# Rows scaled by ScalarE and added in device memory, and squares summed by VectorE, at the end of a transformer layer

## Chip, cores and metric

The kernel runs on one core of a Trainium2 chip. The metric is the device time of one execution in microseconds (us); smaller is better. A time is the median of several runs; beside it stands one profiled execution, whose trace is what the text quotes. Engines are named as in the profile: PE (TensorE), DVE (VectorE), ACT (ScalarE), POOL (GpSimd) and SP (SyncE, here used only to issue transfers). The transfers that SP and ACT issue go through hardware queues, those of POOL through the software queue.

## The reference

One layer of a hybrid encoder on 512 positions of width 1024, in float32. Its first half makes x1 from x. Its second half is a gated MLP with a convolution over positions, and a normalised residual; the end of that second half is where the change lies:

```python
def _rmsnorm(x, g):
    y = x * lax.rsqrt(jnp.mean(x * x, axis=-1, keepdims=True) + EPS)
    return y * g
...
h2 = _rmsnorm(x1, g_pre_ffn)
z  = _conv_gated_mlp(h2, w_up, conv_w, conv_b, w_down)     # ends with (512 x 2816) @ (2816 x 1024)
y  = x1 + _rmsnorm(z, g_post_ffn)
```

For one row of z the end is thus: a sum of 1024 squares, its mean plus EPS to the power -0.5 (one number per row, called the scale here), the product of z, the scale and g_post_ffn, and the sum with x1.

## The kernel before

The 512 positions are four **tokens** in the kernel's words, blocks of 128 rows, one row per partition (NT = 4). The 1024 columns are two halves of 512 (n = 0 and 1). Everything is float32, and a product is made exact enough by splitting each operand in a high and a low part and adding three matmuls.

x1 is made in `norms` (L1138) at some 425 to 455 us, and each half of each token (128 x 512) goes to a scratch tensor in device memory by a transfer of POOL (L1155), since it is needed again only at the very end.

The last product (by `w_down`) is made in two passes, one per half of the output columns. Each pass combines seven products of quarter blocks per step (`products`, a scheme with fewer multiplications; L1358) into the accumulators M1 to M8, and some rest of the contraction is added directly by `add_whole` (L1378), 24 matmuls of 128 x 256 for each token and pass. The first pass leaves its results (columns 0 to 511) in the tiles `c4`. During the second pass `first_share` (L1436) squares and sums those columns on ACT and puts their product with g_post_ffn into the tile `zg[t]`, both well before the end.

What follows the second pass is the **tail**, in `token` (L1452), called for the tokens 0, 2, 1, 3 in this order. For each: `add_whole` finishes the accumulators on PE, first the one for columns 512 to 767 (12 matmuls), then the one for columns 768 to 1023. For each of these two pieces i = 0, 1 of 128 x 256:

- `sums(i)`: DVE adds accumulator and a tile into `z` (L1470), and ACT squares it with a sum along the row (L1472, an ACTIVATE and the read of its accumulator).
- `weighted(i)`: DVE multiplies `z` by g_post_ffn into `zs` (L1477).

Then `first_sum` (L1480) and `scale` (L1487) add up the four sums of squares on DVE, tiny instructions of 128 x 1, and POOL raises the result to the power -0.5 into `qr` (L1488, the pow). `rows` (L1513) makes the result: one DVE instruction per half multiplies `zg` or `zs` by the scale and adds x1, loaded back by SP (L1458), all of it 128 x 512 (the second half of the last token in two pieces of 256), and SP and ACT issue the transfers to the output (L1523). `rows` of one token is called within `token` of the next one, so that it does not wait for its own pow; only the last token's rows stand alone at the end (L1546).

Within one engine, instructions run in the order of the queue. A scheduler sets that order by priority, except where `keep_in_program_order` pins an instruction to the place in which the code gives it, or `issue_after` holds it behind another.

Of the kernel before, what the change touches and what calls it, by code (L numbers as in the profile page):

```python
# [12 lines left out]
AF = mybir.ActivationFunctionType  # L13
# [3 lines left out]
D = 1024  # L17
# [9 lines left out]
NW = 146  # L27
SV0, U0, GATE0, GATE1 = 24, 32, 40, 72
LOOK = 4
NBLK = 66  # L30
WARM = 17
RES_OUT = 6
# [20 lines left out]
def tile_block(ctx: ExitStack, tc, xT, x, wall, par, cs, wsp, bsp, gpost, gffn, out):  # L53
# [33 lines left out]
    def halves(n):  # L87
        return [blk(n=n), blk(n=n)]
# [1361 lines left out]
    ahead = []  # L1450

    def token(t):  # L1452

        if not ww:
            ww.extend([w_get(), w_get()])
        xt = halves("x1")
        for n in range(2):
            nc.sync.dma_start(xt[n], x1[t][n])  # L1458
        add_whole(m, t, (0, 1), ww, True)
        z, zs_ = blk(n="z"), blk(n="zs")  # L1460
        last, ahead[:] = list(ahead), []
        banks = (((M2, e1), (M3, xx)), ((M4, uu), (M8, yy)))[t // 2]
        halves_ = slice(0, 256), slice(256, 512)
        end = t in (1, NT - 1)
        pin = tc.keep_in_program_order if end else (lambda i: i)

        def sums(i):
            b, e = banks[i]
            f = halves_[t % 2]
            pin(v.tensor_add(z[:, halves_[i]], m[b][:, f], e[:, f]))  # L1470
            j = tmp("junk")
            nc.scalar.activation(  # L1472
                out=j[:, :256], in_=z[:, halves_[i]], func=AF.Square, scale=D ** -0.5, accum_out=qn[t][:, 2 + i : 3 + i]
            )

        def weighted(i):
            pin(v.tensor_mul(zs_[:, halves_[i]], z[:, halves_[i]], gpf[1][:, halves_[i]]))  # L1477

        def first_sum():
            pin(v.scalar_tensor_tensor(  # L1480
                out=qn[t][:, 0:1], in0=qn[t][:, 2:3], scalar=EPS, in1=qn[t][:, 0:1], op0=ALU.add, op1=ALU.add
            ))

        sc, s_2 = small("qr", 1, 4), small("qs", 1, 4)

        def scale():
            pin(v.tensor_add(s_2, qn[t][:, 0:1], qn[t][:, 3:4]))  # L1487
            nc.gpsimd.tensor_tensor(out=sc, in0=s_2, in1=nhalf[:, 0:1], op=ALU.pow)  # L1488

        sums(0)  # L1490
        if t == NT - 1:
            weighted(0)
            sums(1)
            first_sum()
            rows(*last, (0,), pin)
            scale()
            rows(*last, (1,), pin)
            weighted(1)
        else:
            weighted(0)  # L1500
            first_sum()
            if end:
                rows(*last, (0,), pin)
            sums(1)
            if last:
                rows(*last, (1,) if end else (0,), pin)
            scale()
            weighted(1)
            if last and not end:
                rows(*last, (1,))  # L1510
        ahead[:] = t, xt, zs_, sc

    def rows(t, xt, zs_, sc, which, pin=lambda i: i):  # L1513

        zt = (zg[t], zs_)
        for i, (a, b) in enumerate(((0, 512), (512, 768), (768, 1024)) if t == NT - 1 else ((0, 512), (512, 1024))):
            if a // S in which:
                f = slice(a % S, a % S + b - a)
                o = zt[a // S][:, f]
                pin(v.scalar_tensor_tensor(  # L1520
                    out=o, in0=o, scalar=sc, in1=xt[a // S][:, f], op0=ALU.mult, op1=ALU.add
                ))
                (nc.sync, nc.scalar)[i % 2].dma_start(out[t, :, a:b], o)  # L1523

    def after6():
        v.tensor_add(uu, m[M6], e1)
# [16 lines left out]
    m[M8] = ps()  # L1543
    for t in (2, 1, 3):
        token(t)
    rows(*ahead, (0, 1))  # L1546


def _parts(a, n, w):
# [129 lines left out]
```

## Time and profile before

| | us |
|---|---|
| median of 3 runs | 783.69 (783.55 to 783.72) |
| profiled execution, its own time | 784.33 |
| its span | 782.6 |
| around the span | 1.73 |
| PE busy | 774.5 (99%) |
| DVE busy | 639.5 (82%) |
| ACT busy | 485.2 (62%) |
| POOL busy | 103.5 (13%) |

The span is what the trace covers, from 0 to 782.6 us; all positions in the text count from its start. The rest of the execution's own time, 1.73 us, lies outside. The profiled execution took 0.64 us more than the median, so a prediction made on the span is carried to the median by its difference. A granted clock of 0.997 in the profiled execution says that PE was hardly throttled.

A row of a timeline gives the start, the duration, engine, line, operation, output and inputs, and in square brackets how long the engine had been idle and what it waited for. Consecutive DVE instructions that don't depend on each other overlap by some 0.08 us in these rows; one that waits for the result of the row ahead starts about 0.03 us after that one's end.

### The profile page before, as it was taken

Reading aid. Unit: us, or ns where it says so; the run is one execution under the profiler, and the core shown is the slowest. Engines: PE = TensorE matmul, PEld = TensorE weight load, DVE = VectorE, ACT = ScalarE, POOL = GpSimd, SP = SyncE. Lnnn points to the kernel's source line nnn. Section 1 sums busy time; section 2 is a strip of 40 time slices with the busy share of each in tenths; the row PEclk is TensorE's granted clock in tenths of the full one; section 3 lists DMA queues with packets and bytes.
Section 4 is the critical chain, followed back from the end, with each engine's and each line's share of the span. In section 5 each row is a group of like instructions: output and inputs, shape, how many; then the busy total and the mean of one; then the engine's idle time right before and its main releaser. Section 6 shows DMA issues by size and latency. Waiting matters only on the chain.

```text
span 782.6 us, 13472 instructions
## 1 busy us (share of the span) xinstructions
PE 774.5 (99%) x5139; PEld 720.7 (92%) x5139; DVE 639.5 (82%) x1093; ACT 485.2 (62%) x878; POOL 103.5 (13%) x132
## 2 busy tenths in 40 slices
PE   9999999999999999999999999999999999999996
PEld 8888998998999999999998998999999998999996
DVE  6567987789789988877765679989999889886987
ACT  7555568688466766644454686657777568644542
POOL 0040001130021102033211200001111012200001
PEclk9999999999999999999999999999999999999998
DMA  8783224453223233233459120435555375733344
GB/s 288 271 246 102 81 82 162 108 122 108 81 91 126 82 122 121 83 110 106 138 171 337 54 81 28 124 107 141 142 148 149 108 199 111 171 114 107 109 162 162
DMA packets 35889, 104.80 MB, mean 134 GB/s; under 512 B 4400, under 2 KB 6320, under 8 KB 35824
## 3 DMA queue, kind: packets, MB, share of 16 engines
q1 hardware_dynamic: 27936, 87.81, 34.0%
q0 software_dynamic: 7024, 14.95, 9.0%
q10 hardware_dynamic: 864, 1.18, 0.4%
q8 instruction: 40, 0.66, 0.4%
q14 instruction: 25, 0.20, 0.1%
HBM read 91.34 MB, written 4.19 MB: 122 GB/s over the span
## 4 chain that ended last, share of the span: by engine, by line
PE 92%; DVE 3%; DMA 3%; issue 1%; ACT 0%; POOLq 0%; DVEq 0%; POOL 0%; ACTq 0%
PE ps L926 24%; PE ps L300 12%; PE ps L302 12%; PE ps L301 12%; PE ps L1372 7%; PE ps L755 5%; PE ps L634 4%; PE ps L636 4%; PE ps L635 4%; DMA raw<-wall 3%; PE ps L1109 2%; PE ps L1108 2%; PE ps L1107 2%; DVE dl L119 1%; PE ps L997 1%
## 5 line engine op out<-in xcount | busy, mean ns | idle before, releaser
L119 DVE TENSOR_TENSOR wl<-raw,wh 128x1024 fp32r<-128x1024 f32 (+1 forms) x84 | 96.0, 1152 | 54.3 <-issue 19.1
L100 ACT ACTIVATE wf<-raw 128x512 fp32r<-128x512 f32 x140 | 85.6, 625 | 67.3 <-PE ps L301 19.4
L926 PE MATMUL ps<-sh,wf 128*128 128x256 f32 x640 | 117.4, 276 | 0.1
L119 DVE TENSOR_TENSOR wf<-raw,wf 128x512 fp32r<-128x512 f32 x140 | 107.0, 774 | 9.2 <-ACT wf L100 8.6
L926 PEld LDWEIGHTS ps<-sh,wf 128*128 128x128 f32 x640 | 101.9, 192 | 1.1 <-ACT sig L100 0.5
L100 ACT ACTIVATE wh<-raw 128x1024 fp32r<-128x1024 f32 (+2 forms) x88 | 84.8, 977 | 28.5 <-DMA raw<-wall 14.0
L300 PE MATMUL ps<-h2h,wh 128*128 128x512 f32 (+1 forms) x256 | 90.6, 354 | 0.0
L301 PE MATMUL ps<-h2l,wh 128*128 128x512 f32 (+1 forms) x256 | 90.4, 353 | 0.0
L302 PE MATMUL ps<-h2h,wl 128*128 128x512 f32 (+1 forms) x256 | 90.4, 353 | 0.0
L926 PE MATMUL ps<-sl,wf 128*128 128x256 f32 x320 | 88.0, 275 | 0.0
L926 PEld LDWEIGHTS ps<-sl,wf 128*128 128x128 f32 x320 | 61.4, 192 | 0.4
L1372 PE MATMUL ps<-dh,fh 128*128 128x256 f32 x216 | 59.6, 276 | 0.3 <-DVE yy L1409 0.3
L1372 PE MATMUL ps<-dl,fh 128*128 128x256 f32 x216 | 59.5, 275 | 0.0
L1372 PE MATMUL ps<-dh,fl 128*128 128x256 f32 x216 | 59.4, 275 | 0.0
L100 ACT ACTIVATE dh<-raw 128x768 fp32r<-128x768 f32 (+1 forms) x36 | 33.6, 950 | 33.8 <-DVE raw L231 15.2
L302 PEld LDWEIGHTS ps<-h2h,wl 128*128 128x128 f32 x256 | 48.6, 190 | 5.1
L301 PEld LDWEIGHTS ps<-h2l,wh 128*128 128x128 f32 x256 | 48.6, 190 | 4.5
L300 PEld LDWEIGHTS ps<-h2h,wh 128*128 128x128 f32 x256 | 48.6, 190 | 4.5
L926 PE MATMUL ps<-xh,wf 128*128 128x256 f32 x288 | 52.2, 275 | 0.0
L636 PE MATMUL ps<-wh,xl 128*128 128x512 f32 x128 | 48.5, 379 | 0.0
L635 PE MATMUL ps<-wl,xh 128*128 128x512 f32 x128 | 48.5, 379 | 0.0
L634 PE MATMUL ps<-wh,xh 128*128 128x512 f32 x128 | 48.5, 380 | 0.0
(343 smaller groups left out, 2171.6 us busy)
## 6 DMA issues: line engine op xcount, KB each, us to landing
raw<-wall SPq DMA_DIRECT2D x144, 512.0 KB, 3.7
x<-x SPq DMA_DIRECT2D x24, 256.0 KB, 6.0
fl<-gp POOLq DMA_DIRECT2D x12, 256.0 KB, 3.8
swap<-qkraw POOLq DMA_DIRECT2D x16, 128.0 KB, 4.8
x<-x POOLq DMA_DIRECT2D x8, 256.0 KB, 2.3
fl<-fs POOLq DMA_DIRECT2D x8, 256.0 KB, 4.3
xT<-xT SPq DMA_DIRECT2D x7, 256.0 KB, 5.0
xT<-xT POOLq DMA_DIRECT2D x4, 256.0 KB, 4.1
```

Of the source, the lines that this page charges most:

```text
L100: return nc.scalar.activation(out=o, in_=i, func=AF.Copy)
L119: low[0] = nc.vector.tensor_sub(lo, src, as32(hi)).ins
L300: nc.tensor.matmul(o, ah, bh, start=start, stop=False, skip_group_check=skip)
L301: nc.tensor.matmul(o, ah, bl, start=False, stop=False, skip_group_check=skip)
L302: pe_last[0] = nc.tensor.matmul(o, al, bh, start=False, stop=stop, skip_group_check=skip).ins
L634: nc.tensor.matmul(acc[t], xh[k][:, c], turns(wh[:, f]), start=k == 0, stop=False)
L635: nc.tensor.matmul(acc[t], xh[k][:, c], turns(wl[:, f]), start=False, stop=False)
L636: part_end[0] = nc.tensor.matmul(acc[t], xl[k][:, c], turns(wh[:, f]), start=False, stop=k == KD - 1)
L755: nc.tensor.matmul(bank[t], a_[:, c], turns(w_[:, f]), start=first and k == i == 0, stop=last and k == 3 and i == 2, skip_group_check=True,)
L926: self.last = nc.tensor.matmul(o, w_[:, c], a_, start=first and k == n == 0, stop=k == 3 and n == 2, skip_group_check=True,)
L1107: nc.tensor.matmul(o, ah, turns(bh), start=k == 0, stop=False)
L1372: nc.tensor.matmul(o, a_[:, c], turns(w_[:, f]), start=j == t == i == 0, stop=j == DP - 1 and i == 2 and n not in (M2, M3, M4), skip_group ...
```

## The change

- **x1 of some rows goes to the output itself.** `norms` writes the halves in `BY_ACT` (both halves of tokens 0 and 2, the first half of token 1) into the output tensor, where x1 then stands until the tail; the other three go to the scratch tensor as before.
- **Those rows are finished by ACT and a transfer that adds.** `scaled_rows`: ACT multiplies the 128 x 512 tile by the scale in place, and POOL issues a transfer to the output with `accum_op=ADD`, which adds it to the x1 that lies there. Their load of x1, the DVE instruction and the transfer of SP or ACT go.
- **The squares of tokens 0, 2 and 1 are summed by DVE** (`squares`: a `tensor_tensor_reduce`, two instructions on the engine: the product with its sum, and the read of the accumulator). The sum starts from the value so far (`scalar=`), so the tiny additions go; EPS is added in `first_share`. For token 3 the first piece is still squared by ACT, the second by DVE.
- **The order at the end of the tail is written anew** for DVE, ACT and POOL.

```diff
+BY_ACT = (0, 0), (0, 1), (2, 0), (2, 1), (1, 0)
...
-            nc.gpsimd.dma_start(x1[t][n], xt[n])
+            nc.gpsimd.dma_start(out[t, :, n * S : (n + 1) * S] if (t, n) in BY_ACT else x1[t][n], xt[n])
...
-        v.tensor_add(qn[t][:, 0:1], qn[t][:, 2:3], qn[t][:, 3:4])
+        v.scalar_tensor_tensor(
+            out=qn[t][:, 0:1], in0=qn[t][:, 2:3], scalar=EPS, in1=qn[t][:, 3:4], op0=ALU.add, op1=ALU.add
+        )
...
-        xt = halves("x1")
+        xt = [None if (t, n) in BY_ACT else blk(n="x1") for n in range(2)]
         for n in range(2):
-            nc.sync.dma_start(xt[n], x1[t][n])
+            if xt[n]:
+                nc.sync.dma_start(xt[n], x1[t][n])
...
+        def squares(i):
             j = tmp("junk")
-            nc.scalar.activation(
-                out=j[:, :256], in_=z[:, halves_[i]], func=AF.Square, scale=D ** -0.5, accum_out=qn[t][:, 2 + i : 3 + i]
-            )
+            pin(v.tensor_tensor_reduce(
+                out=j[:, :256], in0=z[:, halves_[i]], in1=z[:, halves_[i]], scale=1.0 / D, scalar=qn[t][:, i : i + 1],
+                op0=ALU.mult, op1=ALU.add, accum_out=(qn[t][:, 1:2], s_2)[i],
+            ))
...
+        half(0)
+        if t == NT - 1:
+            j = tmp("junk")
+            squared = nc.scalar.activation(
+                out=j[:, :256], in_=z[:, halves_[0]], func=AF.Square, scale=D ** -0.5, accum_out=qn[t][:, 2:3]
+            ).ins
+            weighted(0)
+            with tc.issue_after(squared):
+                scaled_rows(*ahead, 0)
+            rows(*ahead, 1, pin)
+        else:
+            squares(0)
+            weighted(0)
+        half(1)
+        if t == NT - 1:
+            pin(v.tensor_add(qn[t][:, 1:2], qn[t][:, 0:1], qn[t][:, 2:3]))
+        squares(1)
+        power = nc.gpsimd.tensor_tensor(out=sc, in0=s_2, in1=nhalf[:, 0:1], op=ALU.pow).ins
+        weighted(1)
+        if t == 1:
+            with tc.issue_after(power):
+                scaled_rows(*kept, 1, True)
+        if t % 2 == 0:
+            scaled_rows(t, xt, zs_, sc, 0)
+            if t:
+                kept[:] = t, xt, zs_, sc
+                nc.scalar.activation(out=zs_, in_=zs_, func=AF.Copy, scale=sc)
+            else:
+                scaled_rows(t, xt, zs_, sc, 1)
+        ahead[:] = t, xt, zs_, sc
+
+    def scaled_rows(t, xt, zs_, sc, n, done=False):
+
+        o = (zg[t], zs_)[n]
+        if not done:
+            nc.scalar.activation(out=o, in_=o, func=AF.Copy, scale=sc)
+        nc.gpsimd.dma_start(out[t, :, n * S : (n + 1) * S], o, accum_op=ALU.add)
+
+    def rows(t, xt, zs_, sc, n, pin=lambda i: i):
+
+        o = (zg[t], zs_)[n]
+        parts = ((0, 256), (256, 512)) if t == NT - 1 and n else ((0, 512),)
+        for i, (a, b) in enumerate(parts):
             pin(v.scalar_tensor_tensor(
-                out=qn[t][:, 0:1], in0=qn[t][:, 2:3], scalar=EPS, in1=qn[t][:, 0:1], op0=ALU.add, op1=ALU.add
+                out=o[:, a:b], in0=o[:, a:b], scalar=sc, in1=xt[n][:, a:b], op0=ALU.mult, op1=ALU.add
             ))
...
+            (nc.scalar if n and i == 0 else nc.sync).dma_start(out[t, :, n * S + a : n * S + b], o[:, a:b])
```

Three places of the engines' queues show what moves. First DVE's queue from token 3's first piece to the end, before. `z_8895` and `zs_8896` are token 3's, `zg_8436` and `zs_8849` token 1's, `zg_8564` token 3's first half, `q_8180` its sums of squares, `qs_8898` the sum handed to POOL:

```order
L1470 TENSOR_TENSOR z_8895<-ps_8241,e_8182 128x256
L1477 TENSOR_TENSOR zs_8896<-z_8895,gpf_8249 128x256
L1470 TENSOR_TENSOR z_8895<-ps_8772,e_8184 128x256
L1480 SCALAR_TENSOR_TENSOR q_8180<-q_8180 128x1
L1520 SCALAR_TENSOR_TENSOR zg_8436<-zg_8436,qr_8850,x_1463_8820 128x512
L1487 TENSOR_TENSOR qs_8898<-q_8180 128x1
L1520 SCALAR_TENSOR_TENSOR zs_8849<-zs_8849,qr_8850,x_1464_8821 128x512
L1477 TENSOR_TENSOR zs_8896<-z_8895,gpf_8249 128x256
L1520 SCALAR_TENSOR_TENSOR zg_8564<-zg_8564,qr_8897,x_1471_8867 128x512
L1520 SCALAR_TENSOR_TENSOR zs_8896<-zs_8896,qr_8897,x_1472_8868 128x256 x2
```

The same place after the change; ISA is the `tensor_tensor_reduce` and the read of its accumulator, `z_8879`, `zs_8880`, `qs_8882` are token 3's, `zs_8838` token 1's, and line numbers are those of the changed kernel:

```order
L1473 TENSOR_TENSOR z_8879<-ps_8241,e_8182 128x256
L1483 TENSOR_TENSOR zs_8880<-z_8879,gpf_8249 128x256
L1528 SCALAR_TENSOR_TENSOR zs_8838<-zs_8838,qr_8839,x_1459_8811 128x512
L1473 TENSOR_TENSOR z_8879<-ps_8770,e_8184 128x256
L1500 TENSOR_TENSOR q_8180<-q_8180 128x1
L1477 ISA junk_8893,qs_8882<-z_8879,q_8180 128x256
L1477 ISA qs_8882 128x1
L1483 TENSOR_TENSOR zs_8880<-z_8879,gpf_8249 128x256
L1528 SCALAR_TENSOR_TENSOR zg_8564<-zg_8564,qr_8881,x_1466_8851 128x512
L1528 SCALAR_TENSOR_TENSOR zs_8880<-zs_8880,qr_8881,x_1467_8852 128x256 x2
```

Of token 1's two row instructions one is left, and it stands ahead of the addition that makes token 3's last piece of `z`, where both stood behind it; between the sum for POOL and the last rows only the weighted product is left.

Second, POOL's queue from the first pow of the tail, after the change (before, the four pow stand there alone, one behind the other). The tokens in the order of the four `qr` are 0, 2, 1, 3; `zg_8372` and `zs_8740` are token 0's, `zg_8500` and `zs_8796` token 2's, `zg_8436` token 1's:

```order
L1502 TENSOR_TENSOR qr_8741<-qs_8742,nhalf 128x1
L1521 DMA out<-zg_8372 128x512
L1521 DMA out<-zs_8740 128x512
L1502 TENSOR_TENSOR qr_8797<-qs_8798,nhalf 128x1
L1521 DMA out<-zg_8500 128x512
L1502 TENSOR_TENSOR qr_8839<-qs_8840,nhalf 128x1
L1521 DMA out<-zs_8796 128x512
L1521 DMA out<-zg_8436 128x512
L1502 TENSOR_TENSOR qr_8881<-qs_8882,nhalf 128x1
```

Five adding transfers have come between the pows; two of them stand directly ahead of the last one.

Third, ACT's queue from the start of the tail, after the change (before, eight squarings and four transfers stand there):

```order
L1520 ACTIVATE zg_8372<-zg_8372,qr_8741 128x512
L1520 ACTIVATE zs_8740<-zs_8740,qr_8741 128x512
L1520 ACTIVATE zg_8500<-zg_8500,qr_8797 128x512
L1511 ACTIVATE zs_8796<-zs_8796,qr_8797 128x512
L1488 ACTIVATE junk_8884,q_8180<-z_8879 128x256
L1520 ACTIVATE zg_8436<-zg_8436,qr_8839 128x512
L1531 DMA out<-zs_8838 128x512
L1531 DMA out<-zs_8880 128x256
```

Five scalings and one squaring have taken the place of the eight squarings, and the scaling of `zg_8436` stands behind token 3's squaring.

More of the change, by code (lines that the diff above doesn't have):

```diff
@@ L1443, in first_share @@
                 v.tensor_mul(zg[t][:, i * 256 : (i + 1) * 256], src, gpf[0][:, i * 256 : (i + 1) * 256])
-        v.tensor_add(qn[t][:, 0:1], qn[t][:, 2:3], qn[t][:, 3:4])
+        v.scalar_tensor_tensor(
+            out=qn[t][:, 0:1], in0=qn[t][:, 2:3], scalar=EPS, in1=qn[t][:, 3:4], op0=ALU.add, op1=ALU.add
+        )
     m, ww = {}, []
     e1, uu, xx, yy = (blk(n="e") for _ in range(4))
-    ahead = []
+    ahead, kept = [], []
     def token(t):
@@ L1455, in token, with half @@
             ww.extend([w_get(), w_get()])
-        xt = halves("x1")
+        xt = [None if (t, n) in BY_ACT else blk(n="x1") for n in range(2)]
         for n in range(2):
-            nc.sync.dma_start(xt[n], x1[t][n])
+            if xt[n]:
+                nc.sync.dma_start(xt[n], x1[t][n])
         add_whole(m, t, (0, 1), ww, True)
         z, zs_ = blk(n="z"), blk(n="zs")
-        last, ahead[:] = list(ahead), []
         banks = (((M2, e1), (M3, xx)), ((M4, uu), (M8, yy)))[t // 2]
         halves_ = slice(0, 256), slice(256, 512)
-        end = t in (1, NT - 1)
-        pin = tc.keep_in_program_order if end else (lambda i: i)
-        def sums(i):
+        pin = tc.keep_in_program_order if t % 2 else (lambda i: i)
+        sc, s_2 = small("qr", 1, 4), small("qs", 1, 4)
+        def half(i):
             b, e = banks[i]
@@ L1476, in weighted @@
         def weighted(i):
             pin(v.tensor_mul(zs_[:, halves_[i]], z[:, halves_[i]], gpf[1][:, halves_[i]]))
-        def first_sum():
+        half(0)
[11 more added lines that the diff above has]
+            weighted(0)
@@ L1482, in first_sum @@
             ))
[L1484 to L1523, printed above, removed]
+            (nc.scalar if n and i == 0 else nc.sync).dma_start(out[t, :, n * S + a : n * S + b], o[:, a:b])
@@ L1545, in tile_block @@
         token(t)
-    rows(*ahead, (0, 1))
+    for n in range(2):
+        rows(*ahead, n)
 def _parts(a, n, w):
```

## The prediction

> **What bounds the kernel now.** I read the page first, then the busy time by stretches at the end, then the timeline of each engine there. The page:
>
> ```profile
> span 782.6 us, 13472 instructions
> PE 774.5 (99%) x5139; PEld 720.7 (92%) x5139; DVE 639.5 (82%) x1093; ACT 485.2 (62%) x878; POOL 103.5 (13%) x132
> ```
>
> PE is busy for 99% of the span: what isn't on PE matters only where PE waits or has ended. Three stretches at the end (limits, length, then busy us and instructions of PE, PEld, DVE, ACT, POOL, the clock, DMA share, GB/s):
>
> ```profile
> 772.00:775.65 3.65, 3.65 (x33) 3.45 (x31) 3.47 (x10) 1.26 (x5) 1.11 (x2) 1.00 1.04 358
> 775.65:779.60 3.95, 0.00 (x0) 0.00 (x0) 3.80 (x10) 0.78 (x4) 0.93 (x1) 0.81 0.59 227
> 779.60:782.60 3.00, 0.00 (x0) 0.00 (x0) 0.00 (x0) 0.00 (x0) 0.00 (x0) 0.50 0.49 175
> ```
>
> PE runs without a gap until 775.65, and 6.95 us follow: 3.95 of work, almost all DVE, and 3.00 in which only transfers run. All that the change touches inside the tail is hidden under PE unless it makes what follows 775.65 start later or last longer. PE's rows give the beat (token 3's two pieces end here):
>
> ```profile
> 774.03 0.28 PE L1388 MATMUL ps<-wh,fl 128*128 128x256 f32 x1
> 775.37 0.28 PE L1388 MATMUL ps<-wh,fl 128*128 128x256 f32 x1
> ```
>
> A piece of `z` comes every 1.34 us, the last two at 774.31 and 775.65. DVE's timeline there, with the tail's first rows ahead of it:
>
> ```profile
> 765.03 0.42 DVE L1470 TENSOR_TENSOR z<-ps,e 128x256 f32<-128x256 f32 x1
> 765.48 0.42 DVE L1477 TENSOR_TENSOR zs<-z,gpf 128x256 f32<-128x256 f32 x1
> ...
> 767.11 0.68 DVE L1531 TENSOR_TENSOR e<-ps,e 128x512 f32<-128x512 f32 x1
> ...
> 767.82 0.69 DVE L1532 TENSOR_TENSOR e<-ps,e 128x512 f32<-128x512 f32 x1
> ...
> 774.56 0.42 DVE L1477 TENSOR_TENSOR zs<-z,gpf 128x256 f32<-128x256 f32 x1
> ...
> 775.69 0.42 DVE L1470 TENSOR_TENSOR z<-ps,e 128x256 f32<-128x256 f32 x1
> 776.03 0.15 DVE L1480 SCALAR_TENSOR_TENSOR q<-q 128x1 f32<-128x1 f32 x1
> 776.09 0.75 DVE L1520 SCALAR_TENSOR_TENSOR zg<-zg,qr,x 128x512 f32<-128x512 f32 x1
> 776.75 0.15 DVE L1487 TENSOR_TENSOR qs<-q 128x1 f32<-128x1 f32 x1
> 776.83 0.74 DVE L1520 SCALAR_TENSOR_TENSOR zs<-zs,qr,x 128x512 f32<-128x512 f32 x1
> 777.49 0.42 DVE L1477 TENSOR_TENSOR zs<-z,gpf 128x256 f32<-128x256 f32 x1
> 778.01 0.75 DVE L1520 SCALAR_TENSOR_TENSOR zg<-zg,qr,x 128x512 f32<-128x512 f32 x1
> 778.68 0.87 DVE L1520 SCALAR_TENSOR_TENSOR zs<-zs,qr,x 128x256 f32<-128x256 f32 x2
> ```
>
> ACT, POOL and SP beside it:
>
> ```profile
> 776.53 0.19 ACT L1472 ACTIVATION_READ_ACCUMULATOR junk<-z 128x1 f32 x1
> ```
>
> ```profile
> 768.01 0.56 POOL L1488 TENSOR_TENSOR qr<-qs,nhalf 128x1 f32<-128x1 f32 x1 [84.90 <-DVE qs L1487]
> 774.79 0.60 POOL L1488 TENSOR_TENSOR qr<-qs,nhalf 128x1 f32<-128x1 f32 x1 [2.27 <-DVE qs L1487]
> 777.05 0.93 POOL L1488 TENSOR_TENSOR qr<-qs,nhalf 128x1 f32<-128x1 f32 x1 [1.66 <-DVE qs L1487]
> ```
>
> ```profile
> 779.58 0.33 SPq L1523 DMA_DIRECT2D out<-zs  x1
> ```
>
> So the chain is: the last `z` (ends 776.11), squared by ACT (776.72), `qs` (ends 776.90), the pow (starts 0.15 later, ends 777.98), token 3's rows from 778.01, its last transfer at 779.58, the end at 782.6, 3.02 later. Token 1's two row instructions (776.09 and 776.83) aren't in it, but one of them runs while the pow does. That pow took 0.93 where others took 0.56 and 0.60.
>
> **The change, step by step.** Durations by form, in the tail (busy, mean ns, idle):
>
> ```profile
> L1477 DVE TENSOR_TENSOR zs<-z,gpf 128x256 f32<-128x256 f32 x8 | 3.4, 423 | 0.2
> L1520 DVE SCALAR_TENSOR_TENSOR zg<-zg,qr,x 128x512 f32<-128x512 f32 x4 | 3.0, 750 | 0.2
> L1520 DVE SCALAR_TENSOR_TENSOR zs<-zs,qr,x 128x256 f32<-128x256 f32 x2 | 0.9, 477 | 0.0
> L1472 ACT ACTIVATE junk<-z 128x256 f32<-128x256 f32 x8 | 3.4, 420 | 11.1 <-DVE z L1470 10.8 <-DVE q L1480 0.3
> L1472 ACT ACTIVATION_READ_ACCUMULATOR junk<-z 128x1 f32 x8 | 1.5, 186 | 0.0
> ```
>
> *The sum of squares on DVE.* No `tensor_tensor_reduce` is in this trace. The nearest rows bound one of 128 x 256: 0.42 from below (two inputs, no scalar) and 0.75 from above (the same form at twice the elements, as if each element took twice as long). I take 0.48, the row that also has two tensors and a scalar; the accumulator's read is taken as the other 128 x 1 instructions on DVE, 0.155.
>
> *DVE within the tail.* Seven of these pairs come, five row instructions of 0.75 go, and tiny ones. One half then costs z 0.42 and 0.03 of waiting (as from 765.03 to 765.48), the squares 0.48 less 0.08 of overlap, the read 0.07, the product 0.34: 1.26 against PE's 1.34. So DVE keeps up until token 3. From 774.34: z to 774.76, product 774.79 to 775.21, token 1's remaining row instruction 775.13 to 775.88. It holds the last `z` back to 775.80, where it was 775.69: **0.11 lost**.
>
> *The last chain.* z ends 776.22, the tiny sum 776.29, the squares run 776.32 to 776.80, the read ends 776.88 (before, `qs` ended 776.90): the lost 0.11 is regained, ACT's two hand-overs having gone. The pow starts 0.15 later, at 777.03, not 777.05.
>
> *The pow.* Its 0.93 falls to what? It started 0.22 after a row instruction of 0.74, which was followed by a product; the one of 0.60 started 0.23 after the start of a product (0.42, row L1477; the product stands at 774.56). After the change it starts 0.23 after the product that begins at 776.80: the same situation. I take 0.60, so it ends at 777.63 and token 3's rows begin at 777.66 instead of 778.01: **0.35 gained**. The bounds are 0.56 and 0.93.
>
> The Trainium skill, SBUF — State Buffer, section "Who interferes with whom", says that a DVE instruction with two SBUF inputs contends with a GpSimd instruction that reads SBUF, and that the second to issue fully blocks until the first finishes. By that rule the new pow would wait for the product's end at 777.22 and then take its 0.56, and the gain would be 0.20. The 0.60 of the pow at 774.79 speaks against a wait for the whole product, and I keep it.
>
> *After the rows.* Three instructions of DVE and three transfers, the same as before; everything moves by 0.35.
>
> *ACT.* Five scalings come; the nearest row is the copy of the same size on the page:
>
> ```profile
> L100 ACT ACTIVATE wf<-raw 128x512 fp32r<-128x512 f32 x140 | 85.6, 625 | 67.3 <-PE ps L301 19.4
> ```
>
> The first four end by some 773.3 and nobody waits for them but POOL. The fifth stands behind token 3's squaring: 774.79, 0.42 and the read to 775.30, then 0.625 to 775.9.
>
> *POOL.* An adding transfer of this kind (into SBUF, L1273) occupies POOL, and lands, as this says (min, median, max), a plain one of x1 as the last line:
>
> ```profile
> L1273 POOL DMA_DIRECT2D fl<-gp x20: 853/868/1545, 500.7 to 673.8; - x20
> DMA to landing us min/median/max: 3.2/4.1/6.5
> ```
>
> ```profile
> x<-x POOLq DMA_DIRECT2D x8, 256.0 KB, 2.3
> out<-zg SPq DMA_DIRECT2D x4, 256.0 KB, 2.1
> ```
>
> Token 1's is issued at 776.0 and holds POOL to 776.87, just ahead of the pow's 777.03: 0.16 of cover. Were it gone, each tenth would move the end by a tenth. It lands at 780.1 by the median, while the last output transfer (779.23 and 2.1) lands at 781.3: hidden, unless an addition in device memory is slower, for which 6.5 is the bound from above (782.5).
>
> *At nothing:* the three loads of x1 that are left can be issued where the first of the four stand (row below), and are needed from 775.1 on; writing x1 to another tensor in `norms` stays the same eight transfers at some 425 to 455 us, under PE; EPS moved into a tiny instruction under PE.
>
> ```profile
> 755.58 1.81 SPq L1458 DMA_DIRECT2D x<-x  x4
> ```
>
> **The sum:** the profiled execution 784.33 - 0.35 = 783.98; less its 0.64 above the median, **783.3**.
>
> **The rivals.**
>
> *DVE falls behind PE.* Decides from a `tensor_tensor_reduce` of 0.56 us, where a half costs PE's 1.34. At the upper bound of 0.75 a half costs 1.535. From the first z at 765.03, six of them and the two additions L1531 and L1532 (1.32 with their waits) bring token 3's first z to 775.56, where PE would allow 774.34: 1.22 late. The last reduce is slower by 0.27, and the 0.35 comes off: 1.14 later than before, 784.8. For it: an operation that this trace doesn't have. Against it: 0.477 and 0.750 for 256 and 512 elements is 1.07 ns per element with a scalar already in, and a reduce of 256 at that rate is the 0.48 taken. The Trainium skill, Vector Engine (DVE) Microarchitecture Reference, section "Points that are easy to get wrong", says that the layout of instructions with two sources and an accumulator halves its throughput with two fp32 sources in SBUF; no run here shows it with the accumulator, and without it these rows disagree. Chance 0.2, part of it below its full price; since each tenth of a us beyond costs seven tenths, from 0.81 us per instruction on (some 0.06 of the 0.2) the kernel is slower by over 0.2%.
>
> *The software queue ends last.* Token 1's issue takes up to 1.545, and the pow starts 0.5 late: 783.9; or its addition lands at 782.5, 0.8 behind the 781.7 of before: 784.5. For it: the adding transfers of the trace spread from 3.2 to 6.5, and none of them adds in device memory. Against it: in the tail no weights are loaded beside it; whether they make the 6.5 isn't shown. Chance 0.15.
>
> *Nothing is gained.* The order does what the diff says, but the pow stays at 0.93 because POOL comes to it straight from a transfer, or what the pow gains DVE loses: 783.6 to 783.8. Chance 0.1.
>
> **How the numbers follow.** My forecast 0.55. About what a measurement of this kernel can tell from no change is 0.2%, 1.57 us: the forecast, the third rival and most of the first two lie within it. Faster by more would need a quarter of the 6.95 us gone, which no row offers: 0.04. Slower by more: 0.06 of the first rival, 0.02 of the second, 0.02 unforeseen, 0.10. Within: 0.86. The range reaches down to a reduce of 0.42 and a pow of 0.56 and no delay by token 1's row (0.6 gained, and 0.2 of spread): 782.9; and up to the first rival's full price: 784.8.
>
> **What would show it.** The two ISA rows at 0.48 and 0.155; the last `z` near 775.8; the last pow at 0.60; token 3's rows from 777.66. A `z` later than 776.5 shows the first rival; a pow that waits for POOL's own transfer, or a software transfer landing after SP's last one, the second. An operation whose time isn't set by its elements would make it wrong.

## The result and the profile after

The changed kernel takes 785.27 us (median of 11 runs, 784.36 to 786.01), the kernel before in the same session 783.35 (11 runs): a ratio of 1.0023, with a 95% interval of 1.0014 to 1.0032. That is 1.92 us slower; 783.3 was predicted, no difference that could be told. The profiled execution took 785.52, with a span of 783.7.

The page of the changed kernel, its span and the engines' busy time:

```profile
span 783.7 us, 13446 instructions
PE 773.8 (99%) x5139; PEld 719.9 (92%) x5139; DVE 639.0 (82%) x1095; ACT 484.5 (62%) x869; POOL 107.6 (14%) x137
```

PE had the same 5139 matmuls and took 773.8 us for them, where it had taken 774.5, so the loss stands behind PE's end. Its last row, from PE's timeline:

```profile
774.49 0.28 PE L1389 MATMUL ps<-wh,fl 128*128 128x256 f32 x1
```

PE ends at 774.77 here and ended at 775.65 before. The profiled executions of this study end PE anywhere from 774.20 to 775.65, and the order of these ends isn't that of the medians; so I compare traces from PE's end on, and call what follows it the **tail**. Two stretches of it, cut at SP's last issue (limits, length, then busy us and instructions of PE, PEld, DVE, ACT and POOL, the clock, DMA share, GB/s):

```profile
774.77:778.60 3.83, 0.00 (x0) 0.00 (x0) 3.01 (x9) 0.28 (x1) 1.44 (x2) 1.00 1.04 195
778.60:783.70 5.10, 0.00 (x0) 0.00 (x0) 0.00 (x0) 0.00 (x0) 0.00 (x0) 0.57 0.51 141
```

The tail lasts 8.93, where it was 6.95: 1.98 more, close to the 1.92 between the medians. The work after PE's end became 0.10 shorter (3.83 for 3.93). What grew is the stretch in which only transfers run: 5.10 after the last issue, where it was 3.02. The busy share of the DMA engines in the work after PE's end is 1.04 (the times of packets overlap a little, so a share can exceed 1); in the stretch from 775.65 of the kernel before it was 0.59. DVE, POOL and SP in the first stretch, each its own timeline:

```profile
773.46 0.42 DVE L1473 TENSOR_TENSOR z<-ps,e 128x256 f32<-128x256 f32 x1
773.92 0.43 DVE L1483 TENSOR_TENSOR zs<-z,gpf 128x256 f32<-128x256 f32 x1
774.26 0.75 DVE L1528 SCALAR_TENSOR_TENSOR zs<-zs,qr,x 128x512 f32<-128x512 f32 x1
774.93 0.42 DVE L1473 TENSOR_TENSOR z<-ps,e 128x256 f32<-128x256 f32 x1
...
775.44 0.48 DVE L1477 CUSTOM_DVE_ANT_0 junk<-z,q 128x256 f32<-128x256 f32 x1
775.86 0.08 DVE L1477 DVE_READ_ACCUMULATOR2_ANT qs<- 128x1 f32 x1
775.86 0.42 DVE L1483 TENSOR_TENSOR zs<-z,gpf 128x256 f32<-128x256 f32 x1
777.03 0.75 DVE L1528 SCALAR_TENSOR_TENSOR zg<-zg,qr,x 128x512 f32<-128x512 f32 x1 [0.76 <-POOL qr L1502]
```

```profile
773.24 0.60 POOL L1502 TENSOR_TENSOR qr<-qs,nhalf 128x1 f32<-128x1 f32 x1
773.80 0.87 POOL L1521 DMA_DIRECT2D out<-zs  x1
775.55 0.86 POOL L1521 DMA_DIRECT2D out<-zg  x1 [0.88 <-ACT zg L1520]
776.11 0.88 POOL L1502 TENSOR_TENSOR qr<-qs,nhalf 128x1 f32<-128x1 f32 x1
```

```profile
777.81 0.34 SPq L1531 DMA_DIRECT2D out<-zg  x1
778.60 0.34 SPq L1531 DMA_DIRECT2D out<-zs  x1
```

DVE kept up with PE, and its sum of squares is the pair CUSTOM_DVE_ANT_0 and the accumulator's read. Token 3's rows begin 2.26 after PE's end (before 2.36). Now the transfers: the view of the DMA engines of the changed kernel from 765 to 790 us. Each digit of its DMA line is the busy share of 0.625 us in tenths, the queues' shares are of 25 us of 16 engines, and the last number of an issue line is the median from issue to landing:

```profile
DMA  0000000966999597998999999510000000000000
...
q0 software_dynamic: 720, 1.31, 37.4%
q10 hardware_dynamic: 288, 0.39, 4.4%
q1 hardware_dynamic: 288, 0.39, 4.3%
...
out<-zs ACTq DMA_DIRECT2D x1, 256.0 KB, 4.7
out<-zg SPq DMA_DIRECT2D x1, 256.0 KB, 4.6
out<-zs ACTq DMA_DIRECT2D x1, 128.0 KB, 4.3
out<-zs SPq DMA_DIRECT2D x1, 128.0 KB, 4.1
```

The same view of the kernel before:

```profile
DMA  0100000069597999995069659700000000000000
...
q10 hardware_dynamic: 576, 0.92, 9.6%
...
out<-zg SPq DMA_DIRECT2D x4, 256.0 KB, 2.1
...
out<-zs ACTq DMA_DIRECT2D x3, 256.0 KB, 2.5
...
out<-zs SPq DMA_DIRECT2D x1, 128.0 KB, 2.1
```

The engines hardly pause from 769.4 until some 781. The software queue (q0, the five adding transfers of POOL) took 37.4% of 25 us, 9.35 us of all 16 engines for 1.31 MB, while the other queues took 2.2 for 0.78 MB. Plain transfers that SP and ACT issue into this need 4.1 to 4.7 to land where they needed 2.1 to 2.5. The last addition itself, issued at 775.55, is the slowest of the five: it lands 6.7 after its issue, at some 782.2, and SP's last output (778.60 and 4.1) at 782.7.

### The profile page after: what moved, and what is told of

The parts are those of the page before. It is cut to its first block, busy times and chain, and to the rows that moved or that the text cites. A ratio compares the mean times of both kernels' runs of the same rounds, so it can differ in the third digit from the quotient of the medians.

```text
span 783.7 us, 13446 instructions
## 1 busy us (share of the span) xinstructions
PE 773.8 (99%) x5139; PEld 719.9 (92%) x5139; DVE 639.0 (82%) x1095; ACT 484.5 (62%) x869; POOL 107.6 (14%) x137
## 4 chain that ended last, share of the span: by engine, by line
PE 95%; DVE 2%; ACT 1%; DMA 1%; issue 0%; POOLq 0%; POOL 0%; DVEq 0%; ACTq 0%
PE ps L927 21%; PE ps L303 12%; PE ps L301 12%; PE ps L302 12%; PE ps L1373 11%; PE ps L756 5%; PE ps L635 4%; PE ps L637 4%; PE ps L636 4%; PE ps L1389 3%; PE ps L1109 2%; PE ps L1108 2%; PE ps L1110 2%; DVE wf L120 1%; PE ps L421 1%; PE ps L998 1%
```

## The experiments

**Theory A:** an adding transfer keeps the DMA engines busy for 1.87 us (9.35 over five), and token 3's outputs, though issued elsewhere, wait behind and among what is left of that work. **Rivals:** the order of DVE, ACT and POOL is what costs (the squares on DVE, or ACT's part), or each adding transfer has a cost of its own wherever it stands. Each median below is of 8 to 11 runs. In the table, *q0* is the software queue's time in 765 to 790 us (its share times 25), *work* goes from PE's last row to SP's last issue, *landing* from there to the end of the span, in the profiled execution. The ratio is to the kernel before in the same session; the medians of that lie between 783.35 and 783.61.

| kernel | adding + plain on q0 | q0 | work | landing | tail | median us (range) | ratio, 95% interval |
|---|---|---|---|---|---|---|---|
| before | 0 | 0 | 3.93 | 3.02 | 6.95 | 783.35 to 783.61 | 1 |
| changed | 5 + 0 | 9.35 | 3.83 | 5.10 | 8.93 | 785.27 (784.36 to 786.01) | 1.0023 [1.0014, 1.0032] |
| a1_plain | 0 + 5 | 3.40 | 3.54 | 3.05 | 6.59 | 783.25 (782.36 to 784.06) | 0.9996 [0.9988, 1.0005] |
| a2_four | 4 + 0 | 7.70 | 3.65 | 3.75 | 7.40 | 784.18 (783.26 to 784.68) | 1.0007 [0.9999, 1.0016] |
| a3_rows | 5 + 0 | 9.63 | 4.46 | 5.02 | 9.48 | 785.48 (784.97 to 786.4) | 1.0026 [1.0017, 1.0036] |
| a4_squares | 0 | 0 | 5.21 | 3.05 | 8.26 | 784.83 (783.99 to 785.63) | 1.0016 [1.0007, 1.0025] |
| b1_token0 | 2 + 0 | 3.65 | 3.89 | 3.36 | 7.25 | 783.79 (783.31 to 784.81) | 1.0002 [0.9993, 1.0012] |
| b2_pool | 0 | 0 | 6.10 | 3.00 | 9.10 | 785.5 (784.72 to 786.31) | 1.0025 [1.0015, 1.0035] |
| b3_late | 2 + 3 | 5.83 | 3.87 | 4.20 | 8.07 | 784.68 (784.15 to 785.36) | 1.0015 [1.0006, 1.0024] |
| c1_early | 3 + 2 | 7.35 | 3.53 | 3.07 | 6.60 | 782.96 (782.52 to 783.69) | 0.9992 [0.9983, 1.0001] |
| c2_three | 3 + 0 | 5.68 | 3.69 | 3.34 | 7.03 | 783.42 (782.67 to 784.8) | 0.9997 [0.9988, 1.0006] |

The tails differ from that of before by what the medians do, within 0.4 us (a3_rows: 0.6), so the tail of one profiled execution is where each time was lost.

### a1_plain: the same order, the transfers plain

```diff
-        nc.gpsimd.dma_start(out[t, :, n * S : (n + 1) * S], o, accum_op=ALU.add)
+        nc.gpsimd.dma_start(out[t, :, n * S : (n + 1) * S], o)
```

> The changed kernel, with the five adding transfers made plain ones (same queue, same bytes, same places; x1 isn't added in those rows, that part of the work is left out). Theory A, the DMA engines: an adding packet of 2 KB holds its engine about 0.23 us in the changed kernel's trace and a plain one 0.09, so five adding transfers take 9 us of all 16 engines and token 3's output waits among them. Then plain ones are over by 777, token 3's last output lands 2.1 us after its issue and not 4.1, the span ends 3.0 us after SP's last issue and not 5.1, and the time is 783.2 (2.0 below the changed kernel, a little below the kernel before). Theory B, the software queue: whatever POOL issues that late ends late or ends the program late. Then the end stays 4.5 us or more behind SP's last issue, and the time at 785. Theory C, the DVE order: the time stays at 785 with the row instructions of token 3 late; the changed kernel's trace speaks against it.

It takes 783.25 us, and the two microseconds are gone. Its DMA engines and its POOL:

```profile
DMA  0100000288200072468750894000000000000000
...
q0 software_dynamic: 400, 1.31, 13.6%
...
out<-zg SPq DMA_DIRECT2D x1, 256.0 KB, 2.1
```

```profile
775.94 0.54 POOL L1521 DMA_DIRECT2D out<-zg  x1 [1.12 <-ACT zg L1520]
776.53 0.61 POOL L1502 TENSOR_TENSOR qr<-qs,nhalf 128x1 f32<-128x1 f32 x1
```

The same bytes at the same places take 3.40 us of the engines, 0.68 for a transfer instead of 1.87, and the engines have gaps again. POOL's plain transfer goes in 80 packets and its adding one in 144 (400 and 720 for five), but the number of packets isn't the price: ACT's plain outputs in the kernel before go in 144 each too (576 for the four of q10) and take 0.69 us for 256 KB. Nor did SP's and ACT's packets get slower beside the additions: q1 and q10 have 4.3% and 4.2% here, 4.3% and 4.4% in the changed kernel for the same bytes. They waited for their turn.

Landing falls by 2.05. The work falls by 0.29 too: POOL's last issue takes 0.54 instead of 0.86, and the pow behind it takes 0.61 instead of 0.88. The two make the 2.34 by which the tails differ. With the addition left out, neither the order of the engines' work nor the software queue is thus a loss; the tail is 0.36 shorter than before.

### a2_four: one adding transfer less

Token 1's first half goes back to DVE, behind the last weighted product.

```diff
-BY_ACT = (0, 0), (0, 1), (2, 0), (2, 1), (1, 0)
+BY_ACT = (0, 0), (0, 1), (2, 0), (2, 1)
...
-            with tc.issue_after(squared):
-                scaled_rows(*ahead, 0)
             rows(*ahead, 1, pin)
...
         weighted(1)
+        if t == NT - 1:
+            rows(*ahead, 0, pin)
```

> The changed kernel with four adding transfers: token 1's first half goes back to DVE and a plain transfer, behind token 3's last weighted product. Theory A: the four take 7.4 us of the engines from about 769.8 on and end near 778, before token 3's output moves (779.2): it lands 2.1 to 2.6 us after its issue. DVE's extra row instruction of 0.67 stands beside the pow and costs up to 0.3. Time 783.4 to 783.8. Theory B: a software transfer is still issued at 773.8, so 784.5 or more.

Measured: 784.18, between what the two theories gave; the interval of its ratio holds 1. Its two stretches:

```profile
774.60:778.25 3.65, 0.00 (x0) 0.00 (x0) 3.59 (x10) 0.00 (x0) 0.60 (x1) 1.00 1.01 210
778.25:782.00 3.75, 0.00 (x0) 0.00 (x0) 0.00 (x0) 0.00 (x0) 0.00 (x0) 0.52 0.51 190
```

The work is as short as hoped (the last pow takes 0.60), but landing is still 0.7 longer than before: four adding transfers, 7.70 us of the engines, aren't done either when token 3's outputs come.

### a3_rows: the rows alone, the squares back on ACT

```diff
-            pin(v.tensor_tensor_reduce(
-                out=j[:, :256], in0=z[:, halves_[i]], in1=z[:, halves_[i]], scale=1.0 / D, scalar=qn[t][:, i : i + 1],
-                op0=ALU.mult, op1=ALU.add, accum_out=(qn[t][:, 1:2], s_2)[i],
-            ))
+            nc.scalar.activation(
+                out=j[:, :256], in_=z[:, halves_[i]], func=AF.Square, scale=D ** -0.5, accum_out=qn[t][:, 2 + i : 3 + i]
+            )
...
-        if t == NT - 1:
-            pin(v.tensor_add(qn[t][:, 1:2], qn[t][:, 0:1], qn[t][:, 2:3]))
+        pin(v.tensor_add(qn[t][:, 1:2], qn[t][:, 0:1], qn[t][:, 2:3]))
         squares(1)
+        pin(v.tensor_add(s_2, qn[t][:, 1:2], qn[t][:, 3:4]))
```

> One part alone: rows by ACT and five adding transfers as in the change, all squares summed by ACT as before. Theory A: the adding transfers are all there, so token 3's output lands 4 us or more after its issue and the time is 785 to 785.5. If the squares on DVE were what costs, 783.4.

Measured: 785.48, no better than the changed kernel. Landing is 5.02, as with the five adding transfers of the changed kernel, and the work is 0.63 longer. Two rows of DVE show most of why:

```profile
773.58 0.16 DVE L1498 TENSOR_TENSOR q<-q 128x1 f32<-128x1 f32 x1 [0.69 <-ACT junk L1477]
...
775.85 0.42 DVE L1473 TENSOR_TENSOR z<-ps,e 128x256 f32<-128x256 f32 x1
```

DVE waits 0.69 for a sum of squares that stands behind two scalings on ACT, gets behind, and makes the last `z` 0.73 after PE's end (775.12), where the changed kernel made it 0.16 after. The squares on DVE thus aren't the loss; they make the work shorter. In the medians (785.48 and 785.27) that difference can't be told.

### a4_squares: the squares alone, all rows by DVE and plain transfers

```diff
-BY_ACT = (0, 0), (0, 1), (2, 0), (2, 1), (1, 0)
+BY_ACT = ()
...
-            with tc.issue_after(squared):
-                scaled_rows(*ahead, 0)
-            rows(*ahead, 1, pin)
+            rows(*ahead, 0, pin)
...
+            if t == 1:
+                rows(*ahead, 0, pin)
...
         weighted(1)
...
+        if t == 2:
+            rows(*ahead, 0)
+        if t:
+            rows(*ahead, 1, pin)
```

> The other part alone: squares summed by DVE as in the change, all rows by DVE with plain transfers as before. Theory A: token 3's output lands 2.1 us after its issue, as before. DVE has five row instructions of 0.67 more than in the change, with some 0.5 us of slack to hide them: token 3's rows start 2.5 to 3 us later than in the change, the time is 785.5 to 786. So the squares alone need the relief of DVE that the adding transfers give.

Measured: 784.83, slower by another way. Landing is 3.05, nothing is wrong with the transfers; but DVE, which now has the squares and all the rows, makes the last `z` 1.7 after PE's end (row below: 777.35 against 775.64) and still has token 1's row to do behind it:

```profile
777.35 0.42 DVE L1473 TENSOR_TENSOR z<-ps,e 128x256 f32<-128x256 f32 x1
...
778.62 0.74 DVE L1522 SCALAR_TENSOR_TENSOR zs<-zs,qr,x 128x512 f32<-128x512 f32 x1
```

So the two parts of the change belong together: with all rows on it, DVE can't keep up with PE and sum the squares too. The delay is smaller than expected: token 3's rows begin 3.64 after PE's end (779.28), 1.38 later than in the changed kernel, not 2.5 to 3. Token 1's row at 778.62 lies beside the last pow (778.51, 0.60), and the accumulator's read (0.08) beside the next instruction, neither of which the expectation had; whether these two make up the whole difference is not shown.

### b1_token0: only the earliest two transfers add

Token 0 alone is finished by adding transfers, the rows of tokens 2 and 1 stay on DVE, and the squares on ACT but for token 3's last piece.

```diff
-BY_ACT = (0, 0), (0, 1), (2, 0), (2, 1), (1, 0)
+BY_ACT = (0, 0), (0, 1)
...
-            squares(0)
+            by_act(0)
             weighted(0)
+            if t == 1:
+                rows(*ahead, 0, pin)
...
+            by_act(1)
+            if t == 1:
+                rows(*ahead, 1, pin)
```

> Made to beat both: only token 0's two halves by ACT and adding transfers, the earliest ones; the rows of tokens 2 and 1 by DVE and plain transfers, one of token 1's ahead of the last z and one beside the last pow; squares by ACT except token 3's last piece, by DVE. Theory A: two adding transfers take 3.7 us of the engines from about 770 and are over by 774.5, long before token 3's output, which lands 2.1 us after its issue; DVE has room for the four row instructions, its last chain is that of the run with four adding transfers (token 3's last transfer issued 3.65 us after PE's end, against 3.93 before). 6.7 us from PE's end to the span's end against 6.95 before: time 783.2 to 783.4, just below the kernel before. Theory B, that a software transfer in the tail costs by itself: 784 or more.

Measured: 783.79, as before, where a gain was expected. Token 3's transfers land in 2.1 to 2.2, so two early additions don't hold them up. But DVE, with a row instruction of token 2 more in each piece of token 1, makes the last `z` at 775.45, 0.40 after PE's end: what the pow gains is lost there. Landing is 0.3 longer than before, of which the transfers' own landing makes 0.1; the rest lies behind the last landing, and its cause stays open.

### b2_pool: POOL adds in SBUF

Tokens 0 and 2 are scaled by ACT and added by POOL to the x1 loaded back, and SP issues plain transfers; the squares stay on DVE.

```diff
-        nc.gpsimd.dma_start(out[t, :, n * S : (n + 1) * S], o, accum_op=ALU.add)
+        nc.gpsimd.tensor_tensor(out=o, in0=o, in1=xt[n], op=ALU.add)
+        nc.sync.dma_start(out[t, :, n * S : (n + 1) * S], o)
```

> The additions of tokens 0 and 2 by POOL in SBUF instead of by transfers (ACT scales, POOL adds the loaded x1 at 1.27 us each by the row of a 128 x 512 addition on POOL in the trace of before, SP issues plain transfers); squares by DVE; token 1's rows by DVE. Theory A: nothing adds in device memory, token 3's output lands 2.1 us after its issue. What it costs instead is POOL's and DVE's use of the same SBUF reads: if they don't hold each other up, 783.2 to 783.5; if each POOL addition holds DVE up in full (5.1 us, with some 0.5 of slack), up to 788. I expect some of it: 785.

Measured: 785.5. Landing is 3.00, but the work takes 6.10. POOL's additions and DVE's rows in the same stretch:

```profile
772.53 1.28 POOL L1520 TENSOR_TENSOR zg<-zg,x 128x512 f32<-128x512 f32 x1 [0.83 <-ACT zg L1519]
...
774.81 1.54 POOL L1520 TENSOR_TENSOR zs<-zs,x 128x512 f32<-128x512 f32 x1
```

```profile
771.65 0.48 DVE L1476 CUSTOM_DVE_ANT_0 junk<-z,q 128x256 f32<-128x256 f32 x1
...
772.85 1.23 DVE L1476 CUSTOM_DVE_ANT_0 junk<-z,q 128x256 f32<-128x256 f32 x1
...
775.68 1.21 DVE L1528 SCALAR_TENSOR_TENSOR zs<-zs,qr,x 128x512 f32<-128x512 f32 x1 [0.46 <-DMA x<-x]
776.82 0.41 DVE L1472 TENSOR_TENSOR z<-ps,e 128x256 f32<-128x256 f32 x1
```

Beside POOL's addition DVE's sum of squares takes 1.23 where it takes 0.48 alone, and a row instruction 1.21 for 0.75. With a load of x1 that came 0.46 late, the last `z` is made 2.62 after PE's end (776.82 against 774.20). The Trainium skill, SBUF — State Buffer, section "Who interferes with whom", has this contention of a DVE instruction with two SBUF inputs and a GpSimd one that reads SBUF; the 1.23 agrees with it.

### b3_late: only the last two transfers add

```diff
+        kw = dict(accum_op=ALU.add) if (t, n) in ((2, 1), (1, 0)) else {}
-        nc.gpsimd.dma_start(out[t, :, n * S : (n + 1) * S], o, accum_op=ALU.add)
+        nc.gpsimd.dma_start(out[t, :, n * S : (n + 1) * S], o, **kw)
```

> The changed kernel with only the last two transfers of POOL adding (token 2's second half, token 1's first), the first three plain (x1 isn't added in those three halves, that part of the work is left out). Theory A in the form that it is the backlog of five which counts: the two start at 775.5, right after their issue, and end near 779.5 and not 781.9, so token 3's output waits little: it lands 2.5 to 3 us after its issue, time 783.6 to 784.0. If one late adding transfer is enough, whatever stands ahead of it: 785.

Measured: 784.68, between the two. Three plain transfers went ahead, so there was no backlog from token 0, and yet landing is 4.20:

```profile
DMA  0000006780002806999999996100000000000000
...
q0 software_dynamic: 528, 1.31, 23.3%
```

The engines idle at 774, are busy again from 774.4 and full from 775 to 780, with a rest until some 780.6. The two late additions need 3.7 us of all engines and token 1's and token 3's outputs 2.2 more: 5.9 in a stretch that begins at 774.4 ends at 780.3 at the earliest. I had counted only what came before them. The second of these additions lands 4.9 after its issue at 775.13, at some 780.0, and SP's last output (778.20 and 3.1) at 781.3. The result fits A, but also a price per adding transfer; the complement decides.

### c1_early: only the first three transfers add

```diff
-        kw = dict(accum_op=ALU.add) if (t, n) in ((2, 1), (1, 0)) else {}
+        kw = dict(accum_op=ALU.add) if (t, n) in ((0, 0), (0, 1), (2, 0)) else {}
```

> The first three software transfers of the tail (both halves of token 0, the first of token 2) add, the last two (token 2's second half, token 1's first) are plain, so x1 is left out of those two halves; everything else is the changed kernel. It is the complement of the run in which only the last two add. Theory A, the DMA engines as one resource with work to finish: from the shares of the software queue in 765 to 790 us, five adding transfers took 9.35 us of all sixteen engines, five plain ones 3.40, so 1.87 and 0.68 each. Here 3 x 1.87 + 2 x 0.68 = 6.97, a share of 27.9%. The three begin at some 769.4 and are done, with what runs beside them, by 776, before token 3's first output transfer: this one then lands 2.1 us after its issue, the span ends 3.05 after SP's last issue, and the tail is that of five plain transfers, 6.6 us: 783.1 to 783.5 us. Theory B, each adding transfer has its share in the loss, whenever it runs (a cost at the memory, or in POOL's issues): three fifths of the changed kernel's loss of 1.92 stay: 784.3 to 784.7. The run with the last two alone lost 1.16, which left both open.

Measured: 782.96, a little below A's range; three fifths of the loss would have been 784.3 or more.

```profile
DMA  0100000096999979699995795000000000000000
...
q0 software_dynamic: 592, 1.31, 29.4%
...
out<-zg SPq DMA_DIRECT2D x1, 256.0 KB, 2.1
```

```profile
778.04 0.34 SPq L1532 DMA_DIRECT2D out<-zg  x1
```

Three adding transfers are in it, more than in b3_late, and they cost nothing: the tail is 6.60, with five plain transfers it was 6.59. The additions begin at 770, and from 778.1 to 779.4, just when token 3's first output has been issued, the engines have gaps again (the 5 and the 7): they had caught up. What counts is how much of the engines' work is left when the last outputs are issued, not how many additions there were.

### c2_three: a whole version after that reading

Only the first three transfers add; the remaining rows of tokens 2 and 1 are DVE's, and ACT squares token 1's first piece to make room.

```diff
-BY_ACT = (0, 0), (0, 1), (2, 0), (2, 1), (1, 0)
+BY_ACT = (0, 0), (0, 1), (2, 0)
...
+        elif t == 1:
+            j = tmp("junk")
+            nc.scalar.activation(
+                out=j[:, :256], in_=z[:, halves_[0]], func=AF.Square, scale=D ** -0.5, accum_out=qn[t][:, 2:3]
+            )
+            weighted(0)
+            rows(*ahead, 1, pin)
...
         weighted(1)
+        if t == NT - 1:
+            rows(*ahead, 0, pin)
```

> A whole version after theory A: only both halves of token 0 and the first half of token 2 are scaled by ACT and added by transfers; the other rows of tokens 2 and 1 are DVE's and leave by plain transfers of SP and ACT. To make room on DVE, token 1's first piece is squared by ACT, the other pieces of tokens 0, 2 and 1 stay with DVE's sum. Theory A: three adding transfers (5.6 us of all sixteen engines from some 769.4) are over by 776, token 3's outputs land in 2.1 us, and from PE's end to SP's last issue it takes 3.65, as in the run with four adding transfers, which had the same last rows: a tail of 6.7, against 6.95 before and 8.93 with five: 783.2 to 783.6, no difference to before that could be told. Rival: DVE gets behind PE by token 2's row instruction (0.66 us in a stretch where a half costs it 1.2 of PE's 1.34) and the last piece of z comes 0.4 late, as in the run with token 0 alone: 783.7 to 784.1. Rival B, a loss per adding transfer: 784.3 or more.

Measured: 783.42, a ratio of 0.9997 with an interval of 0.9988 to 1.0006: the loss is gone, and the gain can't be told from none. Its last `z` is made at 775.07, 0.20 after PE's end, its outputs land in 2.0 to 2.1. Landing is 0.3 longer than before, as in b1_token0, and its cause stays open here too.

## Why the prediction failed

**The step that failed is *After the rows*:** "Three instructions of DVE and three transfers, the same as before; everything moves by 0.35". The three transfers were the same, and issued 0.25 later than forecast (SP's last 3.83 after PE's end, where 779.23 less 775.65 makes 3.58; that is the pow, below). But they landed 2.0 to 2.5 later than the 2.1 that the step kept. The step took a transfer's 2.1 as its property. It is the time of a transfer that finds the engines with gaps, as in the kernel before and in a1_plain and c1_early, and the change had filled them. The prediction had given 0.10 to any loss of over 0.2%.

**Behind it stands *POOL*.** It asked when an adding transfer itself lands, took the median of 4.1, found that before the last output's landing, called it "hidden", and left the 6.5 to a rival. It didn't ask what the transfer uses. The trace of before had a hint in its view of the DMA engines, at three adding transfers of 256 KB into SBUF, from 580.5 to 586 us:

```profile
DMA packets 441, 0.82 MB, mean 148 GB/s; under 512 B 53, under 2 KB 53, under 8 KB 440
...
q0 software_dynamic: 432, 0.79, 82.8%
```

And at four plain ones of x1 to device memory, from 441 to 456 us:

```profile
q0 software_dynamic: 320, 1.05, 17.9%
```

82.8% of 5.5 us over three makes 1.5 us of all engines for one, and 17.9% of 15 over four 0.67. By the 1.5, five additions from 769.4 with 2.2 of other transfers would have kept the engines until 779.1 without a pause (an estimate from these shares); some 1.5 of the 2.2 are token 3's own outputs, so without them the engines would be done at 777.6, about when the first of these is issued (777.81). By the 1.87 that an addition took in device memory the two sums are 780.9 and 779.5, and the outputs find 1.7 us of work ahead of them. So the trace of before could have shown that the engines come near to being the bound, but not the whole delay, and no rival contained it. *The software queue ends last* had the right culprit and only part of the effect. It let the addition land after the outputs, at 782.5 in the span and 784.5 by the median, with the outputs landing as before. In fact the last addition landed at some 782.2, 6.7 after its issue and so beyond the bound of 6.5, and the outputs, on the same engines, were held up to 782.7; the time is 785.27.

The Trainium skill, DMA: Bandwidth & Descriptors, section "Issuing engines are not separate DMA queues", says that transfers run on the same 16 engines whichever engine issued them, and interleave. The 4.1 to 4.7 of SP's and ACT's transfers beside POOL's agree with it, and c1_early shows that they land in 2.1 once POOL's are done.

**The pow** was mis-sized. 0.35 was to be gained by 0.60 for 0.93; it took 0.88, and the work became 0.10 shorter. The rival *Nothing is gained* had this right: the pow comes to POOL straight behind a transfer. The prediction had put token 1's issue 0.35 after PE's end (776.0 against 775.65); it began at 0.78 (775.55 against 774.77). ACT was as early as forecast, but from the end of its scaling (774.34 and 0.71) to POOL's issue 0.50 pass, where the prediction had allowed 0.1 (775.9 and 776.0). POOL's issue lasts until 776.41, the last sum is read by 775.94, and the pow ends 0.58 after the issue does: its row begins 0.30 before the issue's end and holds that wait. Where the issue is shorter (a1_plain, 0.54) or goes (a2_four), the pow takes 0.60 to 0.61 and the gain is there: a1_plain's tail is 0.36 shorter than before.

**What held.** *The sum of squares on DVE*: 0.48 was taken, and the groups by form have

```profile
L1477 DVE CUSTOM_DVE_ANT_0 junk<-z,q 128x256 f32<-128x256 f32 x7 | 3.4, 485 | 0.2
L1520 ACT ACTIVATE zg<-zg,qr 128x512 f32<-128x512 f32 x3 | 2.2, 717 | 9.2 <-POOL qr L1502 9.2
```

The read was overestimated: 0.08 instead of 0.155, and the product begins with it, so that it costs nothing. *DVE within the tail*: it kept up, and token 1's row held the last `z` back (774.26 and 0.75, then `z` at 774.93), as forecast. The rival *DVE falls behind PE* has no place here: its reduce would have had to take 0.56 or more. The halved throughput of the Trainium skill's Vector Engine (DVE) Microarchitecture Reference, section "Points that are easy to get wrong", doesn't show with both sources in SBUF and an accumulator: 0.485 for 256 elements, against the 0.477 of before without one. Whether this custom instruction has the layout that the section names isn't shown. Nor did the pow wait for a whole product, the rule that the prediction weighed: in a1_plain it began 0.23 after the product (776.30, until 776.72) and took 0.61. *ACT*'s scalings took 0.71 and not 0.625; the last one ended 0.28 after PE's end where 0.25 was forecast, since it begins 0.09 before the end of the accumulator's read ahead of it.

## What to carry to other kernels

A transfer that leaves an engine's instruction queue still needs the DMA engines, so price it in engine time (share of the queue times the window, over the transfers), not only by its own landing. Near the end, add up that time for all that is issued from some point on: where it reaches past the issue of the last outputs, expect them to land later, whoever issued them. In this kernel three additions cost nothing while the engines could catch up before the last outputs (c1_early), and two cost over 1 us as the last transfers ahead of them (b3_late).

## What the runs showed of the hardware

- An adding transfer of 256 KB to device memory takes 1.83 to 1.93 us of all 16 DMA engines (two, three, four and five of them, with no plain one on that queue: 3.65, 5.68, 7.70 and 9.35 or 9.63; in c1_early, less its two plain ones, 2.0), a plain one of the software queue 0.68, one of ACT's hardware queue 0.69.
- Beside that work the plain transfers of SP and ACT land in 4.1 to 4.7 us instead of 2.1 to 2.5, while their packets take no longer (4.3% and 4.4% of the engines against 4.3% and 4.2%).
- POOL is held by the issue of an adding transfer for 0.86 to 0.93 us, of a plain one for 0.54 to 0.61. The row of an adding one directly behind another is 1.22 long, but begins 0.31 before the other's end (768.87, where the first runs from 768.25 to 769.18), so it holds POOL 0.91 more.
- From the end of ACT's scaling to the start of POOL's transfer of that tile, where POOL was idle, 0.35 to 0.38 us pass for the first halves of tokens 0 and 2 and 0.45 to 0.52 for token 1's, with plain and adding ones; why token 1's takes longer is not shown.
- The accumulator's read on DVE (0.08 us) lies wholly beside the next instruction.
